# Small softmax copies shared between GpSimd and VectorE, and the value projection run two token tiles at a time

## The chip, the core and the metric

The kernel runs on one core of one Trainium2 chip. A core has a matrix engine (TensorE, PE in the rows), a vector engine (VectorE, DVE), an activation engine (ScalarE, ACT), a general engine (GpSimd, POOL) and a queue engine (SyncE, SP) that starts transfers. They run side by side, each working through its own list of instructions in order, and wait for each other through semaphores. The metric is the device time of one execution in microseconds (us).

## What is computed

Two layers of a decoder trunk over 512 tokens and 1024 channels, everything in fp32. In each layer a normalized and modulated input h is multiplied with a wide matrix. From the product come queries, keys and values of dilated-window attention (three groups of heads with dilation 1, 4 and 16; four heads of 128 in each), the inputs of a retention branch, and gates. What matters here is the attention and how its three groups are joined:

```python
for g, (window, dil) in enumerate(ATT_PATTERNS):      # (128,1), (512,4), (2048,16)
    o, lse = dilated_window_attention(qa[:, :, g], ka[:, :, g], va[:, :, g], window, dil)
    outs.append(o)
    lses.append(lse)
wts = jax.nn.softmax(jnp.stack(lses, axis=0), axis=0)
o_att = jnp.sum(wts[..., None] * jnp.stack(outs, axis=0), axis=0)
...
merged = sigmoid(ga) * (y_att @ w_proj_attn) + sigmoid(gr) * (y_ret @ w_proj_ret)
return x + gate[:, None, :] * (merged @ w_out)
```

## The kernel before, in words

**Products in three parts.** Every fp32 operand x is split (`split`, L155) into hi, a copy rounded to a shorter format that ScalarE makes, and lo = x - hi, which VectorE makes. A product is then three matmuls: hi·hi, hi·lo, lo·hi (`mm3`, L184). A weight tile comes by DMA into a buffer `wst` and is split into `wh` and `wl`. There are 7 buffers `wst` and 4 each of `wh` and `wl`: `wh25` can be written only when the last matmul that reads `wh21` is over. Accumulators lie in the matrix engine's result memory: 4 of the kind `mm`, 2 `aux` and 2 `po`.

**Projections.** `proj_T` (for queries and keys) keeps weights stationary and moves h through; one call is 2 accumulators of 24 matmuls, on two weight tiles of 4 K tiles each. `values(g)` (for the values of groups 1 and 2) is the other way round: h is stationary, 512 weight columns move; one call has 4 weight tiles of 2 K tiles each, and 4 token tiles, each with an accumulator of 24 matmuls, one token tile after the other. Each token tile goes through all four weight tiles.

**Attention of a head pair.** `scores` makes the masked scores (tiles `s`) and their row maxima. `softmax(pr)` takes exponentials on ScalarE (L526, L531), brings the maxima and sums of group 0 into the token order of groups 1 and 2 with 16 copies of 32 rows (L535, into `mlc`), works out a factor for each group and row (L538 to L549), brings the factors of group 0 back with 16 copies (L552, into `f0`), and multiplies the scores with the factors: for head 0 on VectorE, for head 1 on GpSimd (L557 to L563). `attend(pr, i)` turns the scaled scores with transposes on the matrix engine (L581), splits them into tiles `pt`, and multiplies with the values.

**Order.** The program of a layer (`layer`, L954 on) calls, for head pair 0: queries, keys and scores of the groups, `values(1)`, `scores(0, 2)`, `softmax(0)`, `values(2)`; then for pair 1 `q(1, 0)`, `attend(0, 0)`, `k(1, 0)`, `attend(0, 1)`, and so on to `softmax(1)`, `ret_q(0)`, `attend(1, 0)`, `ret_k(0)`, `attend(1, 1)`. That is the order in which instructions are written. A scheduler then places each engine's instructions into its final list, by priority and by a simulated time line; `tc.high_priority(offset=n)` moves what stands in it ahead by n places in priority. On the chip every engine follows its list strictly: an instruction that waits holds up all behind it.

Tiles are numbered in the order of writing. In layer 0, `values(2)` has the accumulators mm25 to mm28 and the weight tiles 21 to 24; `q(1, 0)`, which follows it, has mm29 and mm30 and the weight tiles 25 and 26; `k(1, 0)` has mm31, mm32 and weight tiles 27 and 28. In layer 1 the same three have mm133 to mm136 (weights 153 to 156), mm137 and mm138 (157, 158), mm139 and mm140.

Of the kernel before, what the change touches and what calls it, by code (L numbers as in the profile page):

```python
# [21 lines left out]
KT = D // P  # L22
# [5 lines left out]
QA, KA, VA, ZA = 0, 1536, 3072, 4608  # L28
QR, KR, VR, ZR = 5120, 6144, 7168, 8192
GA, GR = 9216, 10240  # L30
CW = 256
# [30 lines left out]
def trunk(ctx, tc, x, c, positions, norm_w, w_ada, b_ada, w_in, ret_gn_w, w_proj_attn, w_proj_ret,  # L62
          w_out, final_norm_w, c_small, c_decay, out):
    nc = tc.nc
# [9 lines left out]
    def T(tag, dt=F32, shape=(P, S)):  # L74
        n_of[tag] = n_of.get(tag, 0) + 1
        return big.tile(list(shape), dt, tag=tag, name=f"{tag}{n_of[tag]}", bufs=NB[tag])

    def T2(tag):

        return T(tag, F32R, (P, 2, S))  # L80

    def PS(tag="mm"):
        n_of[tag] = n_of.get(tag, 0) + 1
        return psp.tile([P, S], F32, tag=tag, name=f"ps_{tag}{n_of[tag]}", bufs=NPS[tag])

    def small(shape, name, bufs=2, dt=F32):
        n_of[name] = n_of.get(name, 0) + 1
        return st.tile(list(shape), dt, tag=name, name=f"{name}{n_of[name]}", bufs=bufs)

    def f(ap):  # L90
        return ap.bitcast(F32)
# [4 lines left out]
    def cls(ap, c):  # L96
        return ap.rearrange("p (n c) -> p c n", c=4)[:, c]
# [55 lines left out]
    def split(src, hi, lo, in_order=False):  # L153

        for ins in (nc.scalar.copy(hi, src), nc.vector.tensor_tensor(lo, src, f(hi), op=ALU.subtract)):  # L155
            if in_order:
                tc.keep_in_program_order(ins)
# [3 lines left out]
    def step():  # L161

        while background and next(background[0], True):
            background.pop(0)

    def weights(src, rows0, nk, j0, width=CW):

        step()
        res, per = [], 4 * CW // width
        for k0 in range(0, nk, per):  # L170
            s_ = T("wst", F32, (P, per, width))
            nc.sync.dma_start(s_, src[rows0 + k0 * P:rows0 + (k0 + per) * P, j0:j0 + width]
                              .rearrange("(k p) j -> p k j", p=P))
            hi, lo = T("wh", F32R, (P, per, width)), T("wl", F32R, (P, per, width))
            split(s_, hi, lo)
            res.append((hi, lo))
        return lambda k, part: res[k // per][part][:, k % per]

    def mm3(ps_ap, pairs, first=True, last=True, skip=False):

        n, i = 3 * len(pairs), 0
        for (ah, al), (bh, bl) in pairs:
            for a, b_ in ((ah, bh), (ah, bl), (al, bh)):
                nc.tensor.matmul(ps_ap, a, b_, start=first and i == 0, stop=last and i == n - 1,  # L184
                                 skip_group_check=skip)
                i += 1
# [116 lines left out]
    class Layer:  # L303
# [8 lines left out]
        def proj_T(self, j0):  # L312

            w = weights(self.win, 0, KT, j0)
            res = []
            for t in range(2):
                cols = slice(t * P, (t + 1) * P)
                ps = PS()
                mm3(ps, [((w(k, 0)[:, cols], w(k, 1)[:, cols]), (self.hh[k], self.hl[k])) for k in range(KT)])
                res.append(ps)  # L320
            return res
# [122 lines left out]

        def values(self, g):

            w = weights(self.win, 0, KT, VA + g * 512, 2 * CW)
            self.v[0, g], self.v[1, g] = [], []
            for i in range(4):
                ps = PS()  # L450
                mm3(ps, [((cls(self.hh[k], i), cls(self.hl[k], i)), (w(k, 0), w(k, 1))) for k in range(KT)])
                t = T2("v" if i < 2 else "y")
                hi, lo = t[:, 0], t[:, 1]
                split(ps, hi, lo)
                for pr in range(2):
                    self.v[pr, g].append((hi[:, pr * CW:(pr + 1) * CW], lo[:, pr * CW:(pr + 1) * CW]))

        def values0(self, pr):
            self.v[pr, 0] = self.proj_tok(VA + pr * 256, blk)
# [51 lines left out]
        def softmax(self, pr):  # L511

            mx = [self.sg[g][1] for g in range(3)]
            ml0 = small([P, 4, 2, 2], "ml0")
            mlc = small([P, 4, 2, 2], "mlc")
# [7 lines left out]
            for i in range(2):  # L523
                for b in range(4):
                    s_ = self.p0(i, b)
                    nc.scalar.activation(s_, s_, AF.Exp, scale=SCALE, bias=nm0[:, b, i:i + 1],  # L526
                                         accum_out=ml0[:, b, i, 1:2])
                for g, l_ in ((1, l1), (2, l2)):
                    for cc in range(4):
                        s_ = self.sg[g][0][i][:, cc]  # L530
                        nc.scalar.activation(s_, s_, AF.Exp, scale=SCALE, bias=nm12[:, cc, i:i + 1],  # L531
                                             accum_out=l_[:, cc, i:i + 1])
            for b in range(4):
                for cc in range(4):
                    nc.vector.tensor_copy(mlc[32 * b:32 * b + 32, cc], ml0[32 * cc:32 * cc + 32, b])  # L535
            e = small([P, 2, 4, 2], "e")
            mm_ = small([P, 4, 2], "mm_")
            nc.vector.tensor_tensor(mm_, mlc[:, :, :, 0], m12, op=ALU.max)  # L538
# [8 lines left out]
            f0c, f12, f0 = small([P, 4, 2], "f0c"), small([P, 4, 2], "f12"), small([P, 4, 2], "f0")  # L547
            nc.vector.tensor_mul(f0c, e[:, 0], l1)
            nc.vector.tensor_mul(f12, e[:, 1], l1)  # L549
            for b in range(4):  # L550
                for cc in range(4):
                    nc.vector.tensor_copy(f0[32 * cc:32 * cc + 32, b], f0c[32 * b:32 * b + 32, cc])  # L552
            for i in range(2):
                eng = nc.gpsimd if i else nc.vector
                for g in (1, 2):
                    s_ = self.sg[g][0][i]
                    eng.tensor_tensor(s_, s_, f12[:, :, i:i + 1].to_broadcast([P, 4, P]), op=ALU.mult)  # L557
                s_ = self.p0(i, 0)
                eng.tensor_tensor(s_, s_, f0[:, 0, i:i + 1].to_broadcast([P, P]), op=ALU.mult)
                s_ = self.p0(i, 1)  # L560
                eng.tensor_tensor(s_, s_, f0[:, 1, i:i + 1].to_broadcast([P, CW]), op=ALU.mult)
                s_ = self.sg[0][0][i][1]
# [509 lines left out]
```

## Time and profile before

| | |
|---|---|
| time, median of 3 runs | 1385.19 us (1383.81 to 1386.28) |
| time of the profiled execution | 1384.5 us |
| its span, first to last instruction | 1382.7 us |
| matrix engine busy | 1324.9 us (96%), 6857 matmuls |
| vector engine busy | 964.7 us (70%) |
| ScalarE, GpSimd busy | 584.7 us (42%), 270.1 us (20%) |
| granted clock of the matrix engine, mean | 0.992 of full speed |

In the rows below, a line of the time line is: start, duration, engine, source line, operation, tile written <- tiles read (buffer numbers left out), shape, count of merged instructions, and in brackets how long the engine had been idle before it and who ended that. Matmuls overlap, so the distance from start to start tells the pace, not the duration.

### The profile page before, as it was taken

Reading aid. Unit: us, or ns where it says so; the run is one execution under the profiler, and the core shown is the slowest. Engines: PE = TensorE matmul, PEld = TensorE weight load, DVE = VectorE, ACT = ScalarE, POOL = GpSimd, SP = SyncE. Lnnn points to the kernel's source line nnn. Section 1 sums busy time; section 2 is a strip of 40 time slices with the busy share of each in tenths; the row PEclk is TensorE's granted clock in tenths of the full one; section 3 lists DMA queues with packets and bytes.
Section 4 is the critical chain, followed back from the end, with each engine's and each line's share of the span. In section 5 each row is a group of like instructions: output and inputs, shape, how many; then the busy total and the mean of one; then the engine's idle time right before and its main releaser. Section 6 shows DMA issues by size and latency. Waiting matters only on the chain.

```text
span 1382.7 us, 18104 instructions
## 1 busy us (share of the span) xinstructions
PE 1324.9 (96%) x6857; PEld 1144.5 (83%) x6857; DVE 964.7 (70%) x1656; ACT 584.7 (42%) x991; POOL 270.1 (20%) x224
## 2 busy tenths in 40 slices
PE   4999999999999999999989999999999999999996
PEld 3779978889889887888768898888989889788875
DVE  5997569686654677767888636566865565878678
ACT  5442533253223235753643325234423223567355
POOL 1200100030120383220230001002121126622124
PEclk9999999999999999999999999999999999999998
DMA  9963146222222337994974322222122222688764
GB/s 313 314 188 125 61 145 191 90 64 83 85 77 86 90 62 179 198 184 155 196 230 153 100 91 77 77 78 90 54 92 90 78 83 71 113 197 199 176 157 102
DMA packets 136647, 179.54 MB, mean 130 GB/s; under 512 B 5936, under 2 KB 97264, under 8 KB 136560
## 3 DMA queue, kind: packets, MB, share of 16 engines
q1 hardware_dynamic: 119152, 144.83, 32.8%
q0 software_dynamic: 17408, 33.56, 14.3%
q8 instruction: 54, 0.88, 0.3%
q14 instruction: 33, 0.27, 0.1%
HBM read 174.17 MB, written 4.19 MB: 129 GB/s over the span
## 4 chain that ended last, share of the span: by engine, by line
PE 73%; DVE 13%; issue 5%; DMA 5%; POOL 3%; ACT 1%; SPq 0%; POOLq 0%; DVEq 0%; ACTq 0%
PE ps_mm L184 62%; PE ps_aux L184 5%; DVE wl L155 3%; DMA wst<-in_w_in 3%; PE ps_po L184 2%; PE ps_po L190 1%; DVE f L552 1%; DVE qk L155 1%; PE ps_aux L581 1%; POOL tmp L846 1%; POOL wst L730 1%; PE ps_aux L190 1%; DMA v<-in_w_ada 1%; DVE pt L947 1%; PE ps_po L191 1%
## 5 line engine op out<-in xcount | busy, mean ns | idle before, releaser
L184 PE MATMUL ps_mm<-h,wh 128*128 128x512 f32 x1664 | 525.4, 394 | 5.8 <-POOL h L301 2.1
L155 DVE TENSOR_TENSOR wl<-wst,wh 128x1024 fp32r<-128x1024 f32 (+1 forms) x266 | 341.5, 1290 | 161.7 <-ACT wh L155 154.5
L155 ACT CAST wh<-wst 128x1024 fp32r<-128x1024 f32 (+1 forms) x266 | 277.5, 1047 | 339.3 <-PE ps_mm L184 252.6
L184 PEld LDWEIGHTS ps_mm<-h,wh 128*128 128x128 f32 x1664 | 311.2, 189 | 69.7 <-POOL h L301 2.7
L184 PE MATMUL ps_mm<-h,wl 128*128 128x512 f32 x832 | 326.6, 393 | 3.6 <-DVE wl L155 3.6
L184 PE MATMUL ps_mm<-wh,h 128*128 128x256 f32 (+1 forms) x1248 | 310.7, 336 | 8.8 <-DVE h L155 2.2
L184 PEld LDWEIGHTS ps_mm<-wh,h 128*128 128x128 f32 x1248 | 236.8, 216 | 25.9 <-ACT h L155 3.4
L184 PE MATMUL ps_mm<-wl,h 128*128 128x256 f32 (+1 forms) x624 | 207.0, 334 | 0.0
L184 PEld LDWEIGHTS ps_mm<-h,wl 128*128 128x128 f32 x832 | 157.1, 189 | 36.2 <-DVE wl L155 4.5
L635 POOL TENSOR_TENSOR tmp<-tmp,tmp 128x512 f32<-128x512 f32 x32 | 49.3, 1555 | 487.4 <-ACT wh L155 262.7
L184 PEld LDWEIGHTS ps_mm<-wl,h 128*128 128x128 f32 x624 | 134.8, 216 | 5.7
L184 PE MATMUL ps_mm<-wh,qk 128*128 128x512 f32 x384 | 121.0, 390 | 2.8 <-DVE s L800 2.3
L184 PEld LDWEIGHTS ps_mm<-wh,qk 128*128 128x128 f32 x384 | 72.0, 188 | 19.2 <-DVE s L800 2.7
L184 PE MATMUL ps_mm<-wl,qk 128*128 128x512 f32 x192 | 73.9, 390 | 0.0
L184 PE MATMUL ps_mm<-wh,s 128*128 128x512 f32 x224 | 72.1, 391 | 0.0
L155 ACT CAST qk<-tmp 128x512 fp32r<-128x512 f32 x60 | 36.5, 621 | 71.3 <-POOL tmp L635 51.1
L155 DVE TENSOR_TENSOR v<-ps_mm,v 128x256 fp32r<-128x256 f32 (+1 forms) x52 | 24.0, 463 | 56.7 <-ACT v L155 56.7
L155 ACT CAST qk<-ps_mm 128x512 fp32r<-128x512 f32 x48 | 27.7, 584 | 82.8 <-PE ps_mm L184 82.8
L212 DVE SCALAR_TENSOR_TENSOR tmp<-pt,sc,tmp 128x256 f32<-128x256 f32 x126 | 58.4, 497 | 0.3
L155 ACT CAST v<-ps_mm 128x256 fp32r<-128x256 f32 (+1 forms) x52 | 21.0, 409 | 84.0 <-PE ps_mm L184 82.8
L730 POOL DMA_DIRECT2D wst<-in_w_in x32 | 38.9, 1232 | 75.3 <-DVE wl L155 67.4
L557 POOL TENSOR_TENSOR s<-s,f 128x512 f32<-128x512 f32 x8 | 9.9, 1262 | 223.4 <-DVE f L549 120.8
(224 smaller groups left out, 1749.5 us busy)
## 6 DMA issues: line engine op xcount, KB each, us to landing
wst<-in_w_in SPq DMA_DIRECT2D x162, 512.0 KB, 3.7
pt<-in_w_ada SPq DMA_DIRECT2D x36, 512.0 KB, 5.2
wst<-in_w_in POOLq DMA_DIRECT2D x32, 512.0 KB, 7.5
wst<-in_w_proj_ret POOLq DMA_DIRECT2D x16, 512.0 KB, 6.7
wst<-in_w_out POOLq DMA_DIRECT2D x16, 512.0 KB, 6.0
wst<-in_w_proj_ret SPq DMA_DIRECT2D x12, 512.0 KB, 5.1
wst<-in_w_out SPq DMA_DIRECT2D x12, 512.0 KB, 4.2
wst<-in_w_proj_attn SPq DMA_DIRECT2D x8, 512.0 KB, 4.4
```

The lines of the kernel that those rows point to most:

```text
L155: for ins in (nc.scalar.copy(hi, src), nc.vector.tensor_tensor(lo, src, f(hi), op=ALU.subtract)):
L184: nc.tensor.matmul(ps_ap, a, b_, start=first and i == 0, stop=last and i == n - 1, skip_group_check=skip)
L190: nc.tensor.matmul(ps_ap, st[0], mv, start=first, stop=False, skip_group_check=skip)
L191: nc.tensor.matmul(ps_ap[:, 0:P], st[1], mv[:, 0], start=False, stop=last, skip_group_check=skip)
L212: nc.vector.scalar_tensor_tensor(acc, w_, c_, acc, op0=ALU.mult, op1=ALU.add)
L552: nc.vector.tensor_copy(f0[32 * cc:32 * cc + 32, b], f0c[32 * b:32 * b + 32, cc])
L557: eng.tensor_tensor(s_, s_, f12[:, :, i:i + 1].to_broadcast([P, 4, P]), op=ALU.mult)
L581: nc.tensor.transpose(blk(ps, j), src, ident)
L635: nc.gpsimd.tensor_tensor(a, a, b_, op=ALU.subtract if i == 0 else ALU.add)
L730: nc.gpsimd.dma_start(t, part(r, c, i), accum_op=ALU.add)
L846: eng.tensor_tensor(t, t, a, op=ALU.subtract)
L947: nc.vector.tensor_tensor(xt[b][:, cols], xt[b][:, cols], t, op=ALU.add)
```

## The change

Three edits. In `softmax`, every second one of the two sets of 16 copies goes to GpSimd, the others stay on VectorE. In `weights`, the split stands under a priority that `values` raises by 600 places. In `values`, the loops are exchanged: two token tiles have their accumulators open together, and for each K tile both get their three matmuls before the next K tile; the two are split when both are done.

```diff
-    def weights(src, rows0, nk, j0, width=CW):
+    def weights(src, rows0, nk, j0, width=CW, early=0):
...
-            split(s_, hi, lo)
+            with tc.high_priority(offset=early):
+                split(s_, hi, lo)
...
-            w = weights(self.win, 0, KT, VA + g * 512, 2 * CW)
+            w = weights(self.win, 0, KT, VA + g * 512, 2 * CW, early=600)
             self.v[0, g], self.v[1, g] = [], []
-            for i in range(4):
-                ps = PS()
-                mm3(ps, [((cls(self.hh[k], i), cls(self.hl[k], i)), (w(k, 0), w(k, 1))) for k in range(KT)])
-                t = T2("v" if i < 2 else "y")
-                hi, lo = t[:, 0], t[:, 1]
-                split(ps, hi, lo)
-                for pr in range(2):
-                    self.v[pr, g].append((hi[:, pr * CW:(pr + 1) * CW], lo[:, pr * CW:(pr + 1) * CW]))
+            for i2 in range(2):
+                pss = [PS(), PS()]
+                for k in range(KT):
+                    for j, ps in enumerate(pss):
+                        i = 2 * i2 + j
+                        mm3(ps, [((cls(self.hh[k], i), cls(self.hl[k], i)), (w(k, 0), w(k, 1)))],
+                            first=k == 0, last=k == KT - 1, skip=True)
+                for ps in pss:
+                    t = T2("y" if i2 else "v")
+                    hi, lo = t[:, 0], t[:, 1]
+                    split(ps, hi, lo)
+                    for pr in range(2):
+                        self.v[pr, g].append((hi[:, pr * CW:(pr + 1) * CW], lo[:, pr * CW:(pr + 1) * CW]))
...
-                    nc.vector.tensor_copy(mlc[32 * b:32 * b + 32, cc], ml0[32 * cc:32 * cc + 32, b])
+                    (nc.gpsimd if cc % 2 else nc.vector).tensor_copy(mlc[32 * b:32 * b + 32, cc], ml0[32 * cc:32 * cc + 32, b])
...
-                    nc.vector.tensor_copy(f0[32 * cc:32 * cc + 32, b], f0c[32 * b:32 * b + 32, cc])
+                    (nc.gpsimd if cc % 2 else nc.vector).tensor_copy(f0[32 * cc:32 * cc + 32, b], f0c[32 * b:32 * b + 32, cc])
```

The edits shift the scheduler's lists in both layers. Three places are shown; in the lists of the change the lines of `softmax` have numbers higher by 6, those of `mm3` by 1.

VectorE in layer 0, from the factors of `softmax(0)` on, before (f0c1 and f121 are the factors, f01 the tile of the copies, s7, s8 and s5 the scores of head 0, wl25 to wl27 weights of `q(1, 0)` and `k(1, 0)`, y7 and v12 splits of values):

```order
L155 TENSOR_TENSOR v12_1472<-ps_mm26_1447,v12_1472 128x512
L546 RECIPROCAL l11_1294<-l11_1294 128x8
L155 TENSOR_TENSOR y7_1500<-ps_mm27_1475,y7_1500 128x512
L548 TENSOR_TENSOR f0c1_1347<-e1_1336,l11_1294 128x8
L549 TENSOR_TENSOR f121_1348<-e1_1336,l11_1294 128x8
L552 COPY f01_1349<-f0c1_1347 32x2 x16
L557 TENSOR_TENSOR s7_980<-s7_980,f121_1348 128x512
L557 TENSOR_TENSOR s8_1254<-s8_1254,f121_1348 128x512
L559 TENSOR_TENSOR s5_759<-s5_759,f01_1349 128x128
L561 TENSOR_TENSOR s5_759<-s5_759,f01_1349 128x256
L563 TENSOR_TENSOR s5_759<-s5_759,f01_1349 128x512
L155 TENSOR_TENSOR wl25_1553<-wst25_1550,wh25_1552 128x1024
```

The same place in the change:

```order
L155 TENSOR_TENSOR v11_1469<-ps_mm25_1419,v11_1469 128x512
L552 RECIPROCAL l11_1294<-l11_1294 128x8
L155 TENSOR_TENSOR v12_1472<-ps_mm26_1420,v12_1472 128x512
L554 TENSOR_TENSOR f0c1_1347<-e1_1336,l11_1294 128x8
L555 TENSOR_TENSOR f121_1348<-e1_1336,l11_1294 128x8
L155 TENSOR_TENSOR wl25_1553<-wst25_1550,wh25_1552 128x1024
L558 COPY f01_1349<-f0c1_1347 32x2 x8
L563 TENSOR_TENSOR s7_980<-s7_980,f121_1348 128x512
L563 TENSOR_TENSOR s8_1254<-s8_1254,f121_1348 128x512
L155 TENSOR_TENSOR wl26_1559<-wst26_1556,wh26_1558 128x1024
L565 TENSOR_TENSOR s5_759<-s5_759,f01_1349 128x128
```

The split wl25 has moved from behind the copies and all five multiplications to ahead of them, wl26 to ahead of the last three; eight copies are left; and the split of mm27, which stood ahead of the factors, is gone from here.

The matrix engine in layer 0, at the start of `q(1, 0)`, before (mm31 is an accumulator of `k(1, 0)`, aux36 takes transposed scores of `attend(0, 0)`):

```order
L184 MATMUL ps_mm29_1562<-h1_96,wh25_1552 128x512
L184 MATMUL ps_mm29_1562<-h5_100,wh25_1552 128x512
L184 MATMUL ps_mm30_1587<-h1_96,wh25_1552 128x512
L184 MATMUL ps_mm30_1587<-h5_100,wh25_1552 128x512
L581 MATMUL ps_aux36_1618<-cs_76,s7_980 128x128
L581 MATMUL ps_aux36_1618<-cs_76,s7_980 128x128 x3
L184 MATMUL ps_mm31_1721<-h1_96,wh27_1711 128x512
L184 MATMUL ps_mm31_1721<-h5_100,wh27_1711 128x512
L184 MATMUL ps_mm29_1562<-h1_96,wl25_1553 128x512
```

The same place in the change:

```order
L185 MATMUL ps_mm29_1562<-h1_96,wh25_1552 128x512
L185 MATMUL ps_mm29_1562<-h5_100,wh25_1552 128x512
L185 MATMUL ps_mm29_1562<-h1_96,wl25_1553 128x512
L185 MATMUL ps_mm29_1562<-h1_96,wh25_1552 128x512
L185 MATMUL ps_mm29_1562<-h5_100,wh25_1552 128x512
L185 MATMUL ps_mm29_1562<-h1_96,wl25_1553 128x512
```

What the scheduler had pulled forward to fill the place (two matmuls of mm30, four transposes, two matmuls of mm31) is back behind: mm29 runs from end to end, then mm30, and the transposes of s7 and s8 follow after all 48.

VectorE in layer 0, some 8 rows behind the copies of `softmax(1)`, before (tmp34 and tmp36 come from GpSimd and belong to `ret_q(0)`, qk33 and qk34 are its result; s9 are scores of group 0; pt37 and pt38 the transposed scores of `attend(1, 0)`):

```order
L155 TENSOR_TENSOR wl46_2951<-wst46_2948,wh46_2950 128x1024
L563 TENSOR_TENSOR s9_1938<-s9_1938,f02_2493 128x512
L155 TENSOR_TENSOR qk33_2741<-tmp34_2736,qk33_2741 128x512
L155 TENSOR_TENSOR qk34_2749<-tmp36_2744,qk34_2749 128x512
L155 TENSOR_TENSOR pt37_2605<-ps_aux62_2600,pt37_2605 128x512
L155 TENSOR_TENSOR pt38_2613<-ps_aux63_2608,pt38_2613 128x512
```

The same place in the change:

```order
L569 TENSOR_TENSOR s9_1938<-s9_1938,f02_2493 128x512
L155 TENSOR_TENSOR wl46_2951<-wst46_2948,wh46_2950 128x1024
L155 TENSOR_TENSOR qk33_2741<-tmp34_2736,qk33_2741 128x512
L155 TENSOR_TENSOR pt37_2605<-ps_aux62_2600,pt37_2605 128x512
L155 TENSOR_TENSOR pt38_2613<-ps_aux63_2608,pt38_2613 128x512
L155 TENSOR_TENSOR qk34_2749<-tmp36_2744,qk34_2749 128x512
```

The splits of pt37 and pt38 have moved ahead of that of qk34; ahead of this piece, eight of the 16 copies of f02 are left.

## Rows read from the trace of the kernel before

**Rows 1.** The page, busy time: us (share of the span) and instructions of each engine

```profile
PE 1324.9 (96%) x6857; PEld 1144.5 (83%) x6857; DVE 964.7 (70%) x1656; ACT 584.7 (42%) x991; POOL 270.1 (20%) x224
```

**Rows 2.** Waits of PE from 100 to 990 us: total, times, longest

```profile
PE ps_mm L184 <- DVE wl L155: 3.6, 2, 2.5
PE ps_aux L581 <- DVE pt L155: 2.3, 2, 1.2
...
PE ps_aux L581 <- DVE s L557: 1.7, 3, 0.8
```

**Rows 3.** Time line of PE in layer 0, start of q(1, 0) behind values(2)

```profile
170.67 1.17 PE L184 MATMUL ps_mm<-h,wh 128*128 128x512 f32 x4
172.05 0.63 PE L581 MATMUL ps_aux<-cs,s 128*128 128x128 f32 x4 [0.21 <-DVE s L557]
...
175.68 0.50 PE L184 MATMUL ps_mm<-h,wl 128*128 128x512 f32 x1 [2.53 <-DVE wl L155]
...
187.41 1.04 PE L581 MATMUL ps_aux<-cs,s 128*128 128x128 f32 x8
```

**Rows 4.** Slices of 1 us: PE busy, granted clock, DMA share, GB/s

```profile
178.00:179.00 1.00, 1.00 (x4) 0.50 0.94 279
...
181.00:182.00 1.00, 1.00 (x6) 1.00 1.08 336
```

**Rows 5.** Time line of PE in layer 1, the same place

```profile
845.70 1.09 PE L184 MATMUL ps_mm<-h,wh 128*128 128x512 f32 x4
...
851.06 0.50 PE L184 MATMUL ps_mm<-h,wl 128*128 128x512 f32 x1 [1.09 <-DVE wl L155]
...
861.19 0.93 PE L581 MATMUL ps_aux<-cs,s 128*128 128x128 f32 x7
```

**Rows 6.** The chain that ended last, matmul runs: start, us, what

```profile
29.43 2.74 PE ps_mm L184 x12
...
98.13 5.47 PE ps_mm L184 x24
```

**Rows 7.** Time line of DVE in layer 0, behind the factors of softmax(0)

```profile
166.29 4.89 DVE L552 COPY f<-f0c 32x2 f32<-32x2 f32 x16
171.21 2.14 DVE L557 TENSOR_TENSOR s<-s,f 128x512 f32<-128x512 f32 x2
...
174.41 3.48 DVE L155 TENSOR_TENSOR wl<-wst,wh 128x1024 fp32r<-128x1024 f32 x3
```

**Rows 8.** Time line of ACT in layer 0, behind the exponentials of softmax(0)

```profile
163.32 0.58 ACT L155 CAST v<-ps_mm 128x512 fp32r<-128x512 f32 x1
...
166.33 1.05 ACT L155 CAST wh<-wst 128x1024 fp32r<-128x1024 f32 x1 [0.87 <-PE ps_mm L184]
```

**Rows 9.** Line L552, 160 to 173 us: duration min/median/max in ns

```profile
L552 DVE COPY f<-f0c x16: 156/162/991, 166.3 to 171.0; 32x2 f32<-32x2 f32 x16
```

**Rows 10.** Groups of POOL by form: count, busy us, mean ns, idle before

```profile
L150 POOL TENSOR_TENSOR rs<-rs_t,mhalf 128x2 f32<-128x2 f32 x16 | 11.8, 747 | 14.4 <-DVE rs_t L148 14.2
...
L561 POOL TENSOR_TENSOR s<-s,f 128x256 f32<-128x256 f32 x4 | 2.5, 616 | 1.8 <-DVE f L552 1.8
L559 POOL TENSOR_TENSOR s<-s,f 128x128 f32<-128x128 f32 x4 | 1.6, 402 | 1.1 <-DVE f L552 0.9
...
L1059 POOL MEMSET const-float32-0.0<- 128x1 f32 x1 | 0.1, 99 | 0.2 <-issue 0.2
```

**Rows 11.** Time lines of DVE and PE in layer 0, behind softmax(1)

```profile
293.76 4.98 DVE L552 COPY f<-f0c 32x2 f32<-32x2 f32 x16
...
306.19 1.28 DVE L155 TENSOR_TENSOR qk<-tmp,qk 128x512 fp32r<-128x512 f32 x2
307.39 1.28 DVE L155 TENSOR_TENSOR pt<-ps_aux,pt 128x512 fp32r<-128x512 f32 x2
...
308.12 1.15 PE L581 MATMUL ps_aux<-cs,s 128*128 128x128 f32 x7 [1.17 <-DVE pt L155]
```

**Rows 12.** Line L535, whole span: duration min/median/max in ns

```profile
L535 DVE COPY mlc<-ml x64: 151/160/167, 102.8 to 908.9; 32x4 f32<-32x4 f32 x64
```

## The prediction

> **What bounds the kernel now.** I read the busy times first: the matrix engine is busy for 1324.9 of 1382.7 us [rows 1], so there is little idle time, and the question is which of it the change can reach. The waits of that engine between 100 and 990 us, sorted by who ended them, come next [rows 2]. Three groups touch the code of the diff: 3.6 us, twice, for `wl` splits by VectorE; 2.3 us, twice, for `pt` splits; 1.7 us, three times, for scaled scores. The time line shows where: at the end of `softmax(0)` and `values(2)`, where `q(1, 0)` begins, in layer 0 [rows 3] and layer 1 [rows 5], and behind `softmax(1)` in each layer (layer 0: [rows 11]). Elsewhere in the attention stages the matrix engine runs without a gap, so nothing that makes VectorE faster there can count.
>
> What the place costs is read from start to start. The pace of `q` matmuls is 5.47 / 24 = 0.228 us [rows 6]. In layer 0, from 170.67 to 187.41, 16.74 us, there are 50 matmuls (the two and two, two of mm31, 22 and 22 more), 11.40 us, and four transposes, at most 0.63 [rows 3]. So **4.7 us** are lost, of which 2.53 + 0.21 are waits; the rest is pace: after the wait the granted clock stood at 0.50 of full speed, 1.2 instead of 2.4 GHz, and was back at 1.00 from 181 us on [rows 4]. In layer 1, from 845.70 to 861.19, 15.49 us hold 50 matmuls, 11.40, and eight transposes, at most 1.26: **2.8 us** lost [rows 5]. Behind `softmax(1)` it is the two waits for `pt`, 2.3 us together [rows 2]. That makes 4.7 + 2.8 + 2.3 = **9.8 us** within reach.
>
> **Why VectorE is late there.** In layer 0 it has the factors at 166.3, does the 16 copies in 4.89 us, the multiplications from 171.21 to 174.4, and only then wl25, which the matrix engine has been waiting for [rows 7]. ScalarE, which must make wh25 first, waits for the matrix engine too: the cast starts at 166.33, because the buffer of wh21 is free only when the fourth token tile has passed it [rows 8].
>
> **The change part by part.**
>
> *Two token tiles by K tile.* The number and shapes of matmuls and weight loads are the same. What moves is when a weight buffer comes free: each of the four tiles is last read in the second pair of token tiles, where it takes 12 of 48 matmuls. The second pair starts about 48 × 0.23 = 11 us before 170.67, at 159.6, so wh21 is free at about 162.4 instead of 166.2, before ScalarE has finished the exponentials at 163.3 [rows 8]. Also v11 and v12 are both done at 159.6, and the factors no longer stand behind the split of mm27. ScalarE then makes the two casts of 0.58 and wh25 in 1.05, done near 165.6; VectorE has the factors near 165.2, and splits wl25 until 166.8 (3.48 / 3 = 1.16 each [rows 7]). The matrix engine wants it at 170.67 + 2 × 0.228 = 171.1: four us to spare. The eviction of two accumulators at once is behind 48 matmuls of the next pair, so its cost is nothing; if that cover were gone, it would be two splits of about 0.6. That consecutive groups of matmuls go to different accumulators could cost pace. The run of 12 at the start, where four accumulators take turns, keeps 2.74 / 12 = 0.228, as the run of 24 with one [rows 6]; I take zero. The unfavourable end, one hundredth of a us on each of 384 value matmuls, would be 3.8 us, the other end a gain of the same size; no row points to either.
>
> *Copies.* Of 16, eight stay on VectorE. Undisturbed they take 0.16 us [rows 12]. In the copies behind the factors the median is 162 ns, but the longest 991 [rows 9]: 16 × 0.162 would be 2.6 us, and the set took 4.89. GpSimd was busy with its own multiplications all the while, and copies of VectorE waited those out. What one such copy costs on GpSimd, no row shows. The lower bound is the 99 ns of its memset, the upper the 747 ns of its power of 128x2; between them, the multiplications of 128 and 256 columns, 402 and 616 ns, extrapolate to 0.19 us at two columns [rows 10]. I take 0.19: a copy is nearer to a multiplication than to a power. The worst arrangement is that each copy of VectorE waits out one of GpSimd: 8 × (0.16 + 0.19) = 2.8 us. Then s7 and s8, 2.14 as before, and wl26, 1.16: ready at 166.8 + 2.8 + 2.1 + 1.2 = 172.9. The matrix engine wants it after the 12 matmuls on wl25 and two on wh26, at 170.67 + 14 × 0.228 = 173.9. It fits by 1 us. In layer 1 the order and durations are the same.
>
> The change adds one wait: the multiplications of s5, the last three on VectorE, need GpSimd's copies too. Behind them stand wl27 and the splits of mm27 and mm28, which `k(1, 0)` needs from 170.67 + 48 × 0.228 = 181.6 on, some 6 us after they would be done. GpSimd's own multiplications, of head 1, come 8 × 0.19 = 1.5 us later; `attend(0, 1)`, which reads them, stands behind `k(1, 0)`. SyncE's list lets one background load pass a weight tile of `values(2)`, which is wanted only after 36 of its matmuls. All three: zero.
>
> The Trainium skill speaks against this part: "SBUF — State Buffer", section "Who interferes with whom", says that GpSimd and VectorE share a pair of ports as an exclusive lock, that an fp32 copy within SBUF may take it, and that the later one blocks for the whole instruction. The stretched copies agree with it, and the sum above already lets every copy wait; without any wait it would end 1.5 us earlier and change nothing, since the matrix engine comes later.
>
> The other set of 16 (`mlc`) lies early in the softmax, far from the place of use, and takes 0.16 each undisturbed [rows 12]. Sharing it relieves VectorE by 1.3 us four times where the matrix engine does not wait: nothing.
>
> *Priority.* The lists show the splits wl21 to wl23 ahead of one eviction and otherwise where they were; no wait hangs on them. Zero.
>
> *Behind `softmax(1)`.* The copies took 4.98 us; the `pt` split started at 307.39, behind two `qk` splits from 306.19 on, and released the transposes at 308.12 [rows 11]. With 2.8 us for the copies everything behind them moves up by about 2.2 us, and the split of pt37 moves ahead of one `qk` split (0.6): ready near 305.3. The matrix engine comes about 0.6 earlier to these transposes, at 306.2 on the same clock of reckoning, so the wait goes and 0.9 us are left. Next late is nothing that I can name.
>
> **The sum.** 9.8 us from the profiled execution's 1384.5 give 1374.7. That execution lies 0.7 below the median of the three runs, so the comparable time is **1375.4**. Waits further on (the joins of the retention products, the output product) are set by distances from the matrix engine's own progress and shift along with it.
>
> **The rivals.** (1) *GpSimd's copies are dear.* If a copy there takes p, wl26 is ready at 171.4 + 8p, and the matrix engine waits from p = 0.31 on; behind `softmax(1)` the bound is the same: 8 × (0.16 + p) exceeds 4.98 - 1.17 from 0.32 on. Four places then lose 4 × (8p - 2.5), which eats the gain at p = 0.62. At the power's 0.747 it is 14 us lost against 9.8 gained: 1375.4 + 14 = 1389. For it: that row, and that a copy from one group of 32 rows to another is not in the trace. Against it: the two multiplications, and that full serialization is the worst case. (2) *Half-way*: p between 0.31 and 0.5, or the wait behind `softmax(1)` stays because `qk33` comes through GpSimd, whose list has the copies ahead. That gives 2 to 6 us back: 1377 to 1382. (3) *The reordered lists meet a new wait of 7 us or more elsewhere*: 1382.4 to 1388. The value projection needs two free accumulators at its start instead of one, and the transposes come later, with the `attend` products behind them; but the matrix engine waits for no accumulator at these places now [rows 3, 5]. (4) *The priority does nothing* is part of the forecast already.
>
> **How the numbers follow.** Forecast, 1373.5 to 1377: 0.60. Rival 2, 1377 to 1382: 0.26. Rival 3 or a small copy price that just cancels, 1382.4 to 1388: 0.07. Rival 1, above 1388: 0.07. The measurement can tell 0.2%, 2.8 us, so "faster" means under 1382.4: 0.60 + 0.26 = 0.86. "Same", 1382.4 to 1388, takes the 0.07 of rival 3, and "slower" the 0.07 of rival 1. The range leaves out rivals 1 and 3 and begins at 1373, which is the forecast less 1.2 for the spread of the runs and another 1.2 in case the transposes, counted at their upper bound, hide more loss. It ends at 1381.5: some of rival 2 stays outside.
>
> **What would show it.** Right: in the profile of the changed kernel the matrix engine has no wait of over 0.3 us for `wl` at the start of `q(1, 0)` in either layer, its clock stays at 1.00 there, the cast of wh25 starts before the second pair of token tiles is through, and the transposes behind `softmax(1)` do not wait. GpSimd's copies have starts about 0.2 us apart. Wrong: starts of copies 0.6 us or more apart with VectorE's copies stretched between them; a wait for wl26 instead of wl25; a pace of value matmuls that differs from before; or the same 9.8 us of waits under other names.

## The result, and the profile after

The changed kernel takes 1373.03 us (median of four runs, 1370.34 to 1373.81), the kernel before beside it 1385.34 (four runs, 1383.81 to 1386.28): a ratio of 0.991, 95% interval 0.9891 to 0.9929, a gain of 12.3 us (9.8 to 15.1). Forecast were 1375.4 and a gain of 9.8. The profiled execution of the changed kernel took 1373.44 us, its span 1371.6; against the profiled one of before that is 11.1 us. In the changed file `softmax` and `mm3` stand a few lines lower: L552 became L558, L535 L541, L557 to L563 L563 to L569, L581 L587, L184 L185.

The waits of the matrix engine come first, total, times and longest. These are the waits of over 1 us between 100 and 990 us that the changed kernel has left:

```profile
PE ps_mm L185 <- DVE s L806: 2.3, 1, 2.3
PE ps_mm L185 <- POOL h L302: 2.2, 2, 1.5
PE ps_mm L185 <- ACT h L155: 1.6, 2, 1.5
PE ps_mm L185 <- DVE h L155: 1.1, 1, 1.1
```

None is for `wl`, `pt` or the scaled scores of `softmax`: the three rows of [rows 2] are gone, not shortened. The time line of the matrix engine in layer 0, where [rows 3] had waits of 0.21 and 2.53 us (start, duration, what):

```profile
170.12 0.70 PE L185 MATMUL ps_mm<-h,wh 128*128 128x512 f32 x2
170.66 0.40 PE L185 MATMUL ps_mm<-h,wl 128*128 128x512 f32 x1
...
181.13 1.03 PE L587 MATMUL ps_aux<-cs,s 128*128 128x128 f32 x8
181.92 0.71 PE L185 MATMUL ps_mm<-h,wh 128*128 128x512 f32 x2
```

`q(1, 0)` starts on wl25 without a break, and all the transposes stand behind it. From 181.13 to 181.92, eight of them cost 0.79 us from start to start; the 1.03 that they show as busy is modelled. VectorE at the same place, as [rows 7]:

```profile
163.18 1.22 DVE L155 TENSOR_TENSOR wl<-wst,wh 128x1024 fp32r<-128x1024 f32 x1
164.31 1.43 DVE L558 COPY f<-f0c 32x2 f32<-32x2 f32 x8
165.77 1.29 DVE L563 TENSOR_TENSOR s<-s,f 128x512 f32<-128x512 f32 x2
166.99 2.07 DVE L155 TENSOR_TENSOR wl<-wst,wh 128x1024 fp32r<-128x1024 f32 x1
```

wl25 is split ahead of the copies, at 163.18 instead of 174.41, and wl26 is ready at 169.1. The matrix engine wants it 14 matmuls behind 170.12, near 173.4: a margin of over 4 us. ScalarE, as [rows 8], makes the cast of wh25 at 162.05, behind the exponentials and two casts of values and without a wait, for wh21's buffer is free by then. The exponentials themselves end 2 us earlier (161.0 instead of 163.2): in before they wait 1.05 us for `nm` from VectorE.

```profile
161.00 0.20 ACT L547 ACTIVATE e<-e 128x16 f32<-128x16 f32 x1
161.11 1.04 ACT L155 CAST v<-ps_mm 128x512 fp32r<-128x512 f32 x2
162.05 1.04 ACT L155 CAST wh<-wst 128x1024 fp32r<-128x1024 f32 x1
```

GpSimd's copies in the same time line, and behind `softmax(1)` the split of `pt` and the transposes that [rows 11] had waiting 1.17 us (VectorE, then the matrix engine):

```profile
163.24 3.27 POOL L558 COPY f<-f0c 32x2 f32<-32x2 f32 x8 [58.85 <-DVE f0c L554]
166.59 3.36 POOL L563 TENSOR_TENSOR s<-s,f 128x512 f32<-128x512 f32 x2
```

```profile
299.54 1.28 DVE L155 TENSOR_TENSOR pt<-ps_aux,pt 128x512 fp32r<-128x512 f32 x2
```

```profile
300.50 0.28 PE L185 MATMUL ps_mm<-wh,h 128*128 128x256 f32 x1
300.62 0.93 PE L587 MATMUL ps_aux<-cs,s 128*128 128x128 f32 x7
```

### The profile page after: what moved, and what is told of

The parts are those of the page before. It is cut to its first block, busy times and chain, and to the rows that moved or that the text cites. A ratio compares the mean times of both kernels' runs of the same rounds, so it can differ in the third digit from the quotient of the medians.

```text
span 1371.6 us, 18119 instructions
## 1 busy us (share of the span) xinstructions
PE 1321.6 (96%) x6857; PEld 1144.2 (83%) x6857; DVE 950.7 (69%) x1592; ACT 582.7 (42%) x991; POOL 292.3 (21%) x288
## 4 chain that ended last, share of the span: by engine, by line
PE 79%; DVE 9%; DMA 4%; issue 3%; POOL 2%; ACT 2%; POOLq 0%; SPq 0%; ACTq 0%; DVEq 0%
PE ps_mm L185 67%; PE ps_aux L185 5%; DMA wst<-in_w_in 3%; DVE wl L155 3%; PE ps_po L185 2%; PE ps_po L191 1%; DVE qk L155 1%; PE ps_aux L587 1%; POOL tmp L852 1%; PE ps_aux L191 1%; ACT wh L155 1%; PE ps_po L192 1%; DMA pt<-in_x 1%; PE ps_aux L930 0%; DVE tmp L952 0%
## 5 line engine op out<-in xcount | busy, mean ns | idle before, releaser
L185 PE MATMUL ps_mm<-h,wh 128*128 128x512 f32 x1664 | 524.1, 394 | 5.8 <-POOL h L302 2.1
L155 DVE TENSOR_TENSOR wl<-wst,wh 128x1024 fp32r<-128x1024 f32 (+1 forms) x266 | 344.5, 1300 | 173.4 <-ACT wh L155 167.8
L185 PEld LDWEIGHTS ps_mm<-h,wh 128*128 128x128 f32 x1664 | 310.2, 189 | 69.2 <-POOL h L302 2.7
L185 PE MATMUL ps_mm<-h,wl 128*128 128x512 f32 x832 | 325.7, 392 | 0.0
L185 PE MATMUL ps_mm<-wh,h 128*128 128x256 f32 (+1 forms) x1248 | 309.8, 335 | 10.7 <-POOL h L302 2.2
L185 PEld LDWEIGHTS ps_mm<-wh,h 128*128 128x128 f32 x1248 | 236.1, 216 | 27.8 <-ACT h L155 3.3
L185 PE MATMUL ps_mm<-wl,h 128*128 128x256 f32 (+1 forms) x624 | 207.0, 333 | 0.0
L185 PEld LDWEIGHTS ps_mm<-h,wl 128*128 128x128 f32 x832 | 156.8, 189 | 31.8
L185 PEld LDWEIGHTS ps_mm<-wl,h 128*128 128x128 f32 x624 | 134.7, 216 | 5.6
L185 PE MATMUL ps_mm<-wh,qk 128*128 128x512 f32 x384 | 122.4, 394 | 2.6 <-DVE s L806 2.3
L185 PEld LDWEIGHTS ps_mm<-wh,qk 128*128 128x128 f32 x384 | 72.8, 190 | 19.5 <-DVE s L806 2.7
L185 PE MATMUL ps_mm<-wl,qk 128*128 128x512 f32 x192 | 74.5, 393 | 0.0
L185 PE MATMUL ps_mm<-wh,s 128*128 128x512 f32 x224 | 72.1, 391 | 0.0
L155 DVE TENSOR_TENSOR qk<-tmp,qk 128x512 fp32r<-128x512 f32 x60 | 46.9, 798 | 12.6 <-ACT qk L155 12.3
L541 POOL COPY mlc<-ml 32x4 f32<-32x4 f32 x32 | 7.1, 221 | 200.3 <-ACT s L532 198.9
```

What stands on the lines that cost most here:

```text
L541: (nc.gpsimd if cc % 2 else nc.vector).tensor_copy(mlc[32 * b:32 * b + 32, cc], ml0[32 * cc:32 * cc + 32, b])
```

## The experiments

They were made in three sets, each on a chip of its own and with its own runs of the kernel before beside it: values_only, copies_only, priority_only and change_again beside 20 runs (median 1384.25 us), before_again, dummy_copies, f0_four_times and f0_all_gpsimd beside 24 (1384.23), dummy_sixteen, no_priority, f0_only and before_third beside seven (1386.74). Since medians of one kernel differ by some 2 us from one set of runs to another, each kernel is also read by its places, from the time line of the matrix engine, start to start: A, from `q(1, 0)` to the next product with blocks of 128x256; B, the stage with the transposes behind `softmax(1)`, from its first product with blocks of 128x256 to the next with 128x512; A1 and B1 the same in layer 1. "Sum" is what the four are shorter than in before_again, "gain" what the runs say, from the ratio, with its 95% interval. "First" is the stage from the first matmul on h to the first value matmul, on which the change does nothing.

```
kernel          A      B      A1     B1     sum    gain (interval)     first
before          87.86  26.16  83.69  26.18  -1.6                       98.3
before_again    86.24  26.20  83.65  26.16   0     -0.8 (-2.6 to 1.0)  98.7
before_third    86.23  26.17  83.65  26.17   0.0                       95.8
changed kernel  83.00  24.63  80.40  24.63   9.6   12.3 (9.8 to 15.1)  98.3
change_again    82.98  24.62  80.41  24.62   9.6   11.8 (9.0 to 14.7)  98.4
values_only     83.07  26.16  80.41  26.17   6.4    6.5 (4.3 to 8.7)   96.5
copies_only     83.18  24.62  80.67  24.63   9.2   10.7 (8.0 to 13.4)  96.4
priority_only   86.23  26.16  80.46  26.16   3.2    4.2 (1.9 to 6.4)   95.7
dummy_copies    86.47  26.14  86.43  26.12  -2.9   -1.2 (-3.5 to 0.8)  95.9
dummy_sixteen   85.07  25.66  84.14  25.66   1.7    6.4 (4.3 to 8.5)   96.4
f0_four_times   83.00  27.77  80.41  29.36   1.7    2.2 (0.4 to 4.2)   95.9
f0_all_gpsimd   82.98  23.31  80.40  23.31   7.2*   8.0 (6.0 to 10.2)  96.2
no_priority     83.00  24.62  80.39  24.62   9.6   12.6 (10.4 to 15.0) 95.7
f0_only         83.04  24.63  80.40  24.63   9.6   13.6 (11.6 to 15.7) 98.4
```

(* its transposes moved into the stage ahead of B and B1, which is 2.5 us longer in each layer; that is taken off.)

**The parts alone.** Does each part cure the places that the prediction gives it? values_only keeps all copies on VectorE:

```diff
-                    (nc.gpsimd if cc % 2 else nc.vector).tensor_copy(f0[...], f0c[...])
+                    nc.vector.tensor_copy(f0[...], f0c[...])
```

> The value projection by K tile with its priority, but all copies left on VectorE. Theory (two causes): the early release of the weight buffers alone clears the two places at softmax(0): the list has wl25 ahead of all 16 copies, and wl26 behind them is ready near 172.9 where the matrix engine wants it near 173.3. Gain there 4.9 + 3.3 = 8.2 us; the two waits of 1.2 us behind softmax(1) stay. About 1376.5 to 1377.5. Rival (copies): VectorE's 16 copies are what makes it late everywhere, so little is gained, 0 to 3 us, and the wait moves from wl25 to wl26.

Measured 1378.01, ratio 0.9953 (0.9937 to 0.9969). A and A1 are cleared, the two waits for `pt` stand as they were. The places are as expected; the time lies 0.5 us above the expected range, which had reckoned place A with the slow clock of the first profile.

copies_only is the kernel before with the copies alone, `mlc` and these:

```diff
-                    nc.vector.tensor_copy(f0[...], f0c[...])
+                    (nc.gpsimd if cc % 2 else nc.vector).tensor_copy(f0[...], f0c[...])
```

> Only the copies shared; the value projection as before. Theory (two causes): the two waits behind softmax(1) go, 1.5 us each by start-to-start distances, 3.1 together. At softmax(0) the buffer of wh21 still comes free late, but wl25 is reached some 2.5 to 3 us earlier, so the wait for it shrinks from 2.5 to under 1 us in layer 0 and from 1.1 to about 0 in layer 1, and the granted clock in layer 0 should hold at 1.00: 3 to 4 of 4.9 and 1 to 2.5 of 3.3 gained. Sum 7 to 9.6, 1376 to 1378. If the loop exchange were the sole cure of softmax(0), only 3 us would be gained: 1382.

Measured 1375.10, ratio 0.9923 (0.9903 to 0.9942): all four places are cleared, A and A1 but for 0.2 to 0.3 us. The copies alone bring nearly all of it.

priority_only is the kernel before with `early` alone:

```diff
-            w = weights(self.win, 0, KT, VA + g * 512, 2 * CW)
+            w = weights(self.win, 0, KT, VA + g * 512, 2 * CW, early=600)
```

> Only the raised priority of the value weights' splits. Theory: no wait hangs on them, 1384.5 to 1386.5, all waits of the kernel before present. Rival: earlier value weights bring 2 us or more.

Measured 1380.61, ratio 0.997 (0.9954 to 0.9986). A, B and B1 keep their waits, but A1 is cleared, which was not expected: in layer 1 VectorE's list now has the first split of `q(1, 0)` ahead of its 16 copies; the kernel before has it behind them in both layers ([rows 7] for layer 0):

```profile
840.21 1.23 DVE L155 TENSOR_TENSOR wl<-wst,wh 128x1024 fp32r<-128x1024 f32 x1 [1.07 <-ACT wh L155]
841.35 4.14 DVE L553 COPY f<-f0c 32x2 f32<-32x2 f32 x16
```

The matrix engine wants it at 844.02. The priority was not nothing by itself.

> The change itself once more, for a closer interval on its gain. The time lines of the two profiles give 11.2 us at the four places and 0.3 beside them: ratio 0.9915 to 0.9922. If the median of 12.3 us is right, 0.991 or less.

Measured 1373.83, ratio 0.9915 (0.9894 to 0.9935); that does not tell the two expected gains apart. The parts overlap: their sums, 6.4, 9.2 and 3.2, make 18.8, together they bring 9.6. A is cured by the values or by the copies, A1 by any of the three, B and B1 by the copies alone.

**What before costs by itself.** The same kernel, profiled again:

> The kernel before, unchanged, profiled once more. Two theories of the stage from the first transposes to the first value matmul, which took 98.3 us in the profiles of before, of the change and of its repetition, and 95.7 to 96.5 us in those of the parts alone. If it varies from execution to execution, this profile need not show 98.3 again (95.5 to 99), and the stage says nothing on the change. If the order of the lists sets it, it is 98.3 within 0.2. Both theories expect the four places as before: 87.9 us from q(1, 0) to the values in layer 0, 83.7 in layer 1, 26.2 behind softmax(1) twice, within 0.1. Ratio to before 1.000.

> The kernel before, unchanged, a third profile. In the first one the granted clock fell to 0.50 behind the wait for wl25 in layer 0 and the place cost 87.9 us from q(1, 0) to the values; in the second the same wait of 2.55 us left it at 1.00, and the place cost 86.2. If the clock's fall is a matter of the execution, this profile shows one of the two numbers in layer 0, and 83.7 or, if it falls there, about 86.4 in layer 1; the waits of 2.5 and 1.1 us stay in any case. The stage up to the values is between 95.5 and 99 us.

Place A costs 86.24 and 86.23, not 87.86. The wait for wl25 is the same, but the granted clock stays up. That wait in the second profile, and the slices of the matrix engine that answer to [rows 4], where the clock stood at 0.50 in the first (busy, clock, DMA share, GB/s; second profile):

```profile
175.39 0.50 PE L184 MATMUL ps_mm<-h,wl 128*128 128x512 f32 x1 [2.55 <-DVE wl L155]
```

```profile
178.00:179.00 1.00, 1.00 (x6) 1.00 0.92 296
181.00:182.00 1.00, 1.00 (x6) 1.00 0.91 264
```

So of the 4.7 us in layer 0, 1.6 were the clock of one execution; the fall from 2.4 to 1.2 GHz follows this wait at times, not always. The first stage is another such matter: 98.3, 98.7 and 95.8 us in one and the same kernel, so it tells nothing of the change.

The clock also tells what the runs show beyond the places. Each run has its mean granted clock on record. At 0.993 the runs of before average 1384.2 us (17 runs) and those of the change, no_priority and f0_only 1373.7 (5); at 0.994 it is 1382.4 (9) and 1372.5 (6). So at one clock they are 10.5 and 9.9 us apart, much as the places say; a fit to all 80 runs gives 10.0, give or take 0.9. But 62 runs of before have a mean clock of 0.9923 and these 18 have 0.9936, and a thousandth goes with some 1.2 us: that is another 1.6 us between the kernels.

**What stretched VectorE's copies.** Of the set of [rows 9], in before, two copies start at 166.29 and 166.47, and then come:

```profile
166.64 0.92 DVE L552 COPY f<-f0c 32x2 f32<-32x2 f32 x1
167.57 0.99 DVE L552 COPY f<-f0c 32x2 f32<-32x2 f32 x1
168.59 0.16 DVE L552 COPY f<-f0c 32x2 f32<-32x2 f32 x1
168.76 0.30 DVE L552 COPY f<-f0c 32x2 f32<-32x2 f32 x1
```

The two long ones lie beside GpSimd's two multiplications of 512 columns, from 166.48 to 168.5:

```profile
166.48 2.06 POOL L557 TENSOR_TENSOR s<-s,f 128x512 f32<-128x512 f32 x2 [102.60 <-issue]
```

In dummy_copies VectorE's list is as before; GpSimd makes eight copies more, into a dead tile, ahead of its multiplications:

```diff
                     nc.vector.tensor_copy(f0[...], f0c[...])
+                    if cc % 2:
+                        nc.gpsimd.tensor_copy(mm_[...], f0c[...])
```

> The kernel before, VectorE's list in its old order with all 16 copies of the factors; GpSimd only makes eight copies more, into a tile that nobody reads, ahead of its multiplications. Theory 1, GpSimd's multiplications hold up VectorE's copies, and not their number: the 16 copies take 2.9 us (16 x 0.18) instead of 4.9, the wait for wl25 in layer 0 shrinks from 2.5 to under 1 us, the waits behind softmax(1) go; 5 to 7 us gained, about 1378 on this chip. Theory 2, the number of copies on VectorE counts, or GpSimd's copies hold them up as much as its multiplications: the set stays at 4.5 us or more, the four stalls stay, 1384.

Measured 1385.46, ratio 1.0009 (0.9994 to 1.0025). The set took 5.14 us: theory 1's number missed. But the single copies show why (VectorE, then GpSimd):

```profile
165.19 0.16 DVE L552 COPY f<-f0c 32x2 f32<-32x2 f32 x1
165.37 1.01 DVE L552 COPY f<-f0c 32x2 f32<-32x2 f32 x1
166.39 0.99 DVE L552 COPY f<-f0c 32x2 f32<-32x2 f32 x1
```

```profile
163.47 1.76 POOL L554 COPY mm<-f0c 32x2 f32<-32x2 f32 x8 [100.92 <-DVE f L549]
165.31 2.05 POOL L559 TENSOR_TENSOR s<-s,f 128x512 f32<-128x512 f32 x2
```

Eleven copies run at 0.16 to 0.20 us beside GpSimd's copies; the twelfth meets its first multiplication at 165.31 and waits it out, the next one the second. Eight copies, 1.8 us, were too few to clear 16 of VectorE's. So dummy_sixteen, with the `if` left out: sixteen on GpSimd.

> As dummy_copies, but GpSimd makes sixteen copies more, into a tile that nobody reads, so that its multiplications begin some 3.5 us later than in the kernel before; VectorE's list is as before, with all 16 copies of the factors. Theory 1, what stretches VectorE's copies are GpSimd's multiplications alone, one copy each: the 16 copies are over before the first of them and take 2.9 us (16 x 0.18) instead of 4.9 to 5.1. Theory 2, sixteen copies on VectorE take 4.5 us or more beside any work of GpSimd. If theory 1 holds, the collisions pass to VectorE's multiplications behind the copies (2.1 us for two, instead of 1.3), and some 2 us are left of each place: behind softmax(1) 24.6 to 25.3 instead of 26.2, in layer 0 about 84.5 instead of 86.2 or 87.9: 1379 to 1382. By theory 2 1384.

Measured 1380.58, ratio 0.9954 (0.9939 to 0.9969). VectorE's copies in layer 0 by line (min/median/max in ns), and the time line of VectorE, then GpSimd's copies:

```profile
L552 DVE COPY f<-f0c x16: 156/160/183, 163.7 to 166.4; 32x2 f32<-32x2 f32 x16
```

```profile
163.71 2.85 DVE L552 COPY f<-f0c 32x2 f32<-32x2 f32 x16
166.59 1.29 DVE L558 TENSOR_TENSOR s<-s,f 128x512 f32<-128x512 f32 x2
...
168.01 0.43 DVE L562 TENSOR_TENSOR s<-s,f 128x256 f32<-128x256 f32 x1
168.36 1.53 DVE L564 TENSOR_TENSOR s<-s,f 128x512 f32<-128x512 f32 x1
169.81 4.95 DVE L155 TENSOR_TENSOR wl<-wst,wh 128x1024 fp32r<-128x1024 f32 x3
```

```profile
163.74 4.41 POOL L553 COPY mm<-f0c 32x2 f32<-32x2 f32 x16 [100.83 <-DVE f0c L548]
```

Theory 1 holds: 2.85 us, with 16 copies still on VectorE and none waiting. The collisions pass to what comes next, the splits above all: 4.95 us for three instead of 3.48 [rows 7]. So none of the four places is cleared: the waits for wl25 and its like in layer 1 are 3.5 us together, and B and B1 keep 25.66, above the 24.6 to 25.3 expected. By the places 1.7 us are won, and 3.3 without the clock's fall to 0.50 in layer 1, if that costs 1.6 as in layer 0 of before:

```profile
849.00:850.00 1.00, 1.00 (x4) 0.50 1.09 364
```

The runs say 6.4; but the seven of before beside it have a mean clock of 0.9906 against 0.9925 here, which at 1.2 us for a thousandth is some 2.3. Under 1 us is left.

**How dear may GpSimd's copies be?** In f0_four_times GpSimd makes each of its eight copies four times:

```diff
+                    for _ in range(4 if cc % 2 else 1):
                         (nc.gpsimd if cc % 2 else nc.vector).tensor_copy(f0[...], f0c[...])
```

> The change, with GpSimd making each of its eight copies of the factors four times, 32 in all. The prediction's reckoning, in which each of VectorE's copies waits out GpSimd's: with 4 x 0.27 = 1.08 us in the place of p, four places lose 4 x (8 x 1.08 - 2.5) = 24.6 us, about 1398. Rival: VectorE's copies do not wait for GpSimd's; its own eight stay at 1.4 us and wl26 is on time, so nothing is lost behind softmax(0) in either layer (83.0 and 80.4 us from q(1, 0) to the values); only behind softmax(1) are GpSimd's multiplications and its products for qk33, 6.5 us later, late, 2 to 4 us twice: 1378 to 1382.

Measured 1381.69, ratio 0.9984 (0.997 to 0.9997). By line, layer 0:

```profile
L559 POOL COPY f<-f0c x32: 176/179/1192, 161.6 to 176.5; 32x2 f32<-32x2 f32 x32
L559 DVE COPY f<-f0c x8: 149/159/164, 162.7 to 163.9; 32x2 f32<-32x2 f32 x8
```

VectorE's eight are not touched by GpSimd's 32, and A and A1 lose nothing. What is late is the last part of the scores, whose multiplication waits for GpSimd; behind `softmax(1)` the matrix engine waits for that:

```profile
299.88 0.44 PE L588 MATMUL ps_aux<-cs,s 128*128 128x128 f32 x2 [0.71 <-DVE pt L155]
...
303.00 0.66 PE L588 MATMUL ps_aux<-cs,s 128*128 128x128 f32 x4 [1.73 <-DVE s L570]
```

3.1 and 4.7 us are lost there against the change; in layer 1 the granted clock fell to 0.50 behind the wait, which is the 1.6 us between the two:

```profile
975.00:976.00 1.00, 1.00 (x7) 0.50 0.00 0
```

The reckoning with the lock (1398) falls; its rival was right in place and, but for the clock, in size.

f0_all_gpsimd is the change with all 16 copies of the factors there:

```diff
-                    (nc.gpsimd if cc % 2 else nc.vector).tensor_copy(f0[...], f0c[...])
+                    nc.gpsimd.tensor_copy(f0[...], f0c[...])
```

> The change, with all 16 copies of the factors on GpSimd. VectorE has none, and waits with the first multiplication of s5 until GpSimd is through, at 163.2 + 16 x 0.27 + 1.1 = 168.6; wl26 stands behind it and is ready near 171.5, the matrix engine wants it at 173.4. If GpSimd's copy takes 0.27 us, it fits: 1373.8, as the change. If 16 in a row take 0.41 each, wl26 is ready near 173 and the margin is used up: a wait of up to 0.5 us, and its clock, 1374 to 1376. Behind softmax(1) GpSimd's products for qk33 come 2.2 us later; pt37 stands ahead of qk33 on VectorE here, so no wait.

Measured 1375.54, ratio 0.9942 (0.9926 to 0.9957). A and A1 are as in the change; wl26 is ready at 165.2 in a profile that stands some 2 us earlier here, so near 167.3 on the change's clock and not near 171.5, for the multiplication ahead of it needs the first copies only, and the two that wait for the rest stand behind it. Some 1.3 us a layer are lost against the change behind `softmax(1)`, where a wait of 0.63 us appears for an output of `attend` (VectorE's L607). Not foreseen.

**What the prediction took for nothing.** no_priority leaves `early` out of the change, f0_only has the first set of copies on VectorE:

```diff
-            w = weights(self.win, 0, KT, VA + g * 512, 2 * CW, early=600)
+            w = weights(self.win, 0, KT, VA + g * 512, 2 * CW)
```

```diff
-                    (nc.gpsimd if cc % 2 else nc.vector).tensor_copy(mlc[...], ml0[...])
+                    nc.vector.tensor_copy(mlc[...], ml0[...])
```

> The change without the priority for the splits of the values' weights. The prediction takes the priority for nothing: 1373.8, the same four places cleared (83.0, 80.4, 24.6 and 24.6 us), as the lists at these places read alike. Rival: the priority alone cleared layer 1's place, so without it a wait comes back somewhere in the value stage: 1 to 3 us more.

> The change, with the first set of 16 copies, mlc, on VectorE alone. The prediction takes sharing these for nothing: 1373.8, the four places as in the change. Rival: the factors come 1.3 us later (8 x 0.16), and with them the splits behind them, so that a part of the places comes back: in layer 0 the margin of wl26 is over 4 us, so nothing; behind softmax(1) the transposes' margin, which no row gives, decides, at most 1.2 us twice: 1374 to 1376.

Measured 1373.10, ratio 0.9909 (0.9892 to 0.9925), and 1372.82, ratio 0.9902 (0.9887 to 0.9916). All four places are those of the change to 0.04 us, so both terms are zero within it. The larger gains stand against a before that was 2.5 us slower; neither kernel is shown to beat the change.

## Why the prediction was right, and where not

**Right: the places and the way.** The forecast named four places and nothing else, and by the profile the change works there and nowhere else: 4.86, 3.29, 1.53 and 1.55 us, 11.2 together, between the two first profiles, whose spans lie 11.1 apart. The stages next to B and B1 add 0.3; the start and the gate stages differ by under 1 us each, with both signs. The buffer of wh21 is free even before the 162.4 that was said (the twelfth of the last 48 value matmuls starts at 161.30), the cast of wh25 is early, the granted clock is 1.00 behind all four places, no new wait has come up, the pace of the value matmuls is unchanged (49.07 and 49.17 us for the stage), and priority and `mlc` are worth nothing inside the change.

**Wrong: the size, by 2.4 us,** 1375.4 against 1373.03. The step that failed is the sum, in two places: its four terms were too small, because the idle time of the waits for `pt` was taken for their cost and the transposes were taken off at their upper bound, and one execution's distance from its median was added.

The first is the four terms, 9.8 instead of 11.2. "2.3 us, twice, for `pt`" is the idle time that the view of waits shows, 1.17 and 1.16; from start to start it is 1.53 and 1.55. In [rows 11] the first transposes behind the wait take 1.15 where they take 0.93 without it, and the idle time is counted from a modelled end: the last matmul ahead of the wait starts at 306.67, its successor at 308.12, 1.45 later, where the pace is 0.12:

```profile
306.67 0.28 PE L184 MATMUL ps_mm<-wh,h 128*128 128x256 f32 x1
```

That is 0.75 us too little. And the transposes of places A and A1, taken off at "at most 0.63" and "at most 1.26", cost 0.79 for eight: so 2.8 should have been 3.3, and 4.7 was 4.86. That is 0.65. The other waits show the same: 2.74 us idle in layer 0 cost 3.24 where the clock holds (86.24 - 83.00).

The second is the step from the profiled execution to the median: 0.7 was added because the profiled execution of before lies that far below its median. The profiled one of the change lies 0.4 above its own. 1.1 us of the miss are that, and such a shift between single executions is not to be forecast from one. The range went down to 1373.0, a gain of 12.2 us on the 1385.19 known then; 12.3 were measured on the before beside it. The 1.2 us set aside for hidden loss were used up by the four terms, which are 1.4 larger.

**A term that held by luck.** The 4.7 us contain 1.6 us of a slow clock, which the text took as part of the place. Two of three profiles of before don't have them, and dummy_copies is 2.8 us longer in layer 1 instead, with the clock at 0.50 there. By the undisturbed profiles the four places are worth 9.6 us, with 0.3 in the stages between 9.9; with the fall in one of three, 10.5. Both lie in the measured interval, at its low end. What the medians show above that goes with the clock: at one clock the runs are 10.0 us apart, and 1.6 more come with the higher mean clock. So the prediction's 1.6 us of clock are near what the change brings by the runs, but it had them from one fall in one profile; its waits alone, 8.2 us, measured 9.6. Whether all of the clock's share comes from falls at the four places is not shown: the first stage and those of the gates, which differ by 2 to 3 us between the three profiles of before, are too loose to tell it.

**Right by a wrong reason: the copies.** The set was reckoned at 2.8 us, each copy of VectorE waiting out one of GpSimd; it took 1.43. Of the 3.5 us by which the set became shorter, 2.0 come because GpSimd, busy with its own copies, starts the multiplications that stretched VectorE's after these are through: dummy_sixteen has that alone, 2.85 us for 16. The other 1.4 are the eight copies that left. For the same reason the thresholds of rival 1, 0.31 and 0.62 us a copy, were not thresholds. At four copies for one, 0.72 us of GpSimd by the median of 179 ns, the reckoning loses 4 x (8 x 0.72 - 2.5) = 13 us; at A and A1 nothing is lost, and at B and B1 6.3 by another wait and 1.6 by the clock. Its price was near: 0.19 was taken, 179 to 194 ns are the medians of the durations, 0.24 us is the distance from start to start. The wait that the change adds, of the last part of the scores for GpSimd, was rightly costed at zero for this dose; it is what the fourfold dose runs into.

The Trainium skill, "SBUF — State Buffer", section "Who interferes with whom", which the prediction weighed against this part, says that the engine that comes first keeps the shared ports for the whole instruction. Copies of VectorE that meet a multiplication of GpSimd agree (0.92 to 1.01 us), and so does GpSimd's first copy, which takes 1.19 us beside a split by VectorE. Copies that meet copies do not show it: 0.16 to 0.20 us on VectorE. Whether they take no lock, or hold it too briefly to be seen, no run here tells.

**Wrong: who cures what.** The forecast gave layer 0 and layer 1 to the values and `softmax(1)` to the copies. The copies alone clear all four places; the values add some 0.5 us to that. The view of waits named VectorE's late splits, and whatever makes them early enough clears a place: at A1 three different edits do.

## What to carry to other kernels

Cost a wait from start to start of the instructions around it, not by its idle time, which left out 0.2 to 0.4 us of each here; and take the place from two profiles, for a fall of the clock behind it may belong to one execution. Where small copies of one engine are stretched, look first at which long instruction of the other they stand beside: moving that one later took 2.0 us off the set here, halving the copies 1.4. But the collision passes to the next long instruction, so moving alone cleared no place. When several parts of a change bring the same split forward, their gains don't add.

## What was not expected of the hardware

A copy of 32x2 on GpSimd takes 179 to 194 ns by the median, nearly as little as VectorE's 160, and beside each other VectorE's take 0.20 us at most. Against a long instruction, one small copy pays for all of it: 0.92 to 1.01 us for a multiplication of 128x512, 1.19 for a split of 128x1024. The loss passes both ways: wl26 took 2.07 us instead of 1.22 beside GpSimd's multiplications, and these 3.36 for two instead of 2.05.

The same wait of 2.5 us at the same place was followed by a granted clock of 0.50 in one profile of a kernel, and of 1.00 in two others. Of the eight profiles in which one of the four places has a wait, four show a fall of the clock behind it; of the six in which none has, none does, and there the length of a place varied by no more than 0.3 us (B and B1 of f0_all_gpsimd aside, whose transposes stand elsewhere).
